# AdaLN beside w_out and the feed-forward network, in steps of four blocks

## The chip, the cores and the metric

The kernel runs on one core of one Trainium2 chip. The metric is the device time of one execution in microseconds (us). The engines of the core are TensorE (PE: matmuls and transposes; PEld: the loading of its stationary operand), VectorE (DVE), ScalarE (ACT), GpSimd (POOL) and SyncE (SP, which here issues the DMAs). Each works through a queue of its own in order, and semaphores tie the queues together.

## What is computed

Two layers of a diffusion backbone. Each layer normalises the tokens, modulates them, mixes them (a state space model, a neighbourhood attention and a grouped-query attention side by side), projects with w_out, and runs a gated feed-forward network. One tile of 128 prompt tokens and four tiles of sample tokens go through, with a width of 1024. Cut to what matters here:

```
m = silu(cond) @ w_ada + b_ada                 # 1024 -> 6 * 1024, for prompt and sample
sh1, sc1, g1, sh2, sc2, g2 = split(m, 6)
h = layer_norm(x) * (1 + sc1) + sh1
o = mixing(h) @ w_out
x = layer_norm(ALPHA * x + g1 * o, ln1_g, ln1_b)
h = layer_norm(x) * (1 + sc2) + sh2
a, gate = split(h @ w_ffn_in, 2)
x = layer_norm(ALPHA * x + g2 * ((silu(a) * gate) @ w_ffn_out), ln2_g, ln2_b)
```

The first three lines' `m` is what is called AdaLN below: six vectors (vec 0 to 5 for sh1, sc1, g1, sh2, sc2, g2) of 1024 numbers for each of two conditions, in each layer.

## The kernel before, in words

All large products are done in fp32 as three passes of matmuls over a high and a low part (`mm3`: lines L311, L312, L313). A weight comes from memory into a raw buffer, ScalarE casts its high part (L283) and GpSimd or VectorE subtracts it for the low part (L284, tile `wl`, `hl` or another).

**AdaLN.** `ada` makes one item: half a vector, 512 columns of `w_ada`. Its 1024 rows come as eight blocks of 128 rows x 512 columns (256 KB each, L377). Each block is multiplied by four small matmuls (L381), so 32 for an item, which add up in one PSUM bank; ScalarE copies the result out (L385), TensorE transposes it ("turns the row", L386), and VectorE adds the bias into `modc` (L391 or L393). After the second half of a gate (vec 2 or 5) the column copy `gc` (L396), another transpose (L398) and a store (L401) put the gate out as a row. With `side=True` the blocks come into the ring `ev` of four buffers, which also holds the low parts of some weights in the turn and the intermediate values of the SSM tables.

**The turn.** `wout` multiplies the groups of token tiles (2, 1, 0) and (3, 4) by w_out, for two halves `n` of the columns each; VectorE applies the gate (L1497) and the residual (L1303), then come the layer norm (L1288, L1298), the transposes to the network's input (L417), the modulation (L423) and differences and splits for the network (`ffn_in_tile`, L1545, L284). After the products of the second group, three items of `ada` are issued (`ADAW`): both halves of vec 5 of this layer, and, in layer 0 only, the first half of vec 0 of layer 1.

**The network.** Its hidden width is cut into 22 slices f = 0 to 21, in six parts of 4, 4, 4, 3, 4 and 3. The first two are "plain": their first halves need tiles 0, 1 and 2 only, their second halves (which end at L1711 and L1712) also tiles 3 and 4. The other slices use seven products of 12 matmuls in the manner of Strassen, with sums on VectorE (L1588 for weights, L1638, L1654 and L1656 for results in `ys`). After each part its w_ffn_out products follow. From f = 2 on each f is followed by one step of `ffn_side`: in layer 0 an item of `ada` for layer 1 (nine items) and a step of the SSM tables of layer 1 (`ssm_tables`: among others the products L615 and sums L617 in `ev`, stored as tabC). Layer 1 has no layer behind it, and so no side work in its network.

Which instruction stands where in an engine's queue is decided by a scheduler ahead of time, from the order of the code and its own estimates of durations; in the network, `issue_after(self.mark.ins)` keeps a side step behind the last VectorE product of its f.

## Time and profile before

| | us |
|---|---|
| three timed runs, median | 1805.65 |
| lowest and highest | 1800.99, 1809.15 |
| the profiled execution | 1804.75 |
| its span in the trace | 1802.7 |
| TensorE busy | 1655.2 (92% of the span) |
| VectorE busy | 1224.2 (68%) |
| ScalarE busy | 822.3 (46%) |
| GpSimd busy | 762.5 (42%) |

The span runs from the first to the last instruction that the profiler saw; 2.05 us of the profiled execution lie around it. Durations below are from this one execution.

### The profile page before, as it was taken

What the parts mean: (1) busy time and instruction counts of PE and PEld (TensorE: products, weight loads), DVE (VectorE), ACT (ScalarE), POOL (GpSimd) and SP (SyncE); (2) the same over time, 40 slices, a digit from 0 to 9 for tenths busy, and PEclk for the clock granted to TensorE, in tenths of its full rate; (3) what the DMA queues carried; (4) which work ended last, traced back from release to release, by engine and by line L of the source; (5) the groups of instructions that cost most, each with busy time, mean ns of one, the idle gap of its engine ahead of it and who ended that gap; (6) DMA issues with size and microseconds to landing.
All of it is one profiled execution on the core that took longest, in us unless ns stands there. A gap on an engine that the chain in (4) does not pass through costs nothing.

```text
span 1802.7 us, 31473 instructions
## 1 busy us (share of the span) xinstructions
PE 1655.2 (92%) x11624; PEld 1447.3 (80%) x11624; DVE 1224.2 (68%) x2460; ACT 822.3 (46%) x1796; POOL 762.5 (42%) x651
## 2 busy tenths in 40 slices
PE   5889899898899999999898989998979999999997
PEld 3778677676688888898797978976759898998995
DVE  5576536646778777678877555565476787876777
ACT  5435445556542334243246446665564342432433
POOL 3753303048434334346266232210684464363453
PEclk8889899889899999999999989998989999999999
DMA  8434767545453545332324243463542232222312
GB/s 311 121 110 116 231 202 203 149 158 178 149 161 115 176 126 184 109 115 72 122 77 165 91 115 86 121 183 113 178 161 83 91 98 64 89 74 68 105 60 82
DMA packets 183114, 234.90 MB, mean 130 GB/s; under 512 B 78960, under 2 KB 112048, under 8 KB 182960
## 3 DMA queue, kind: packets, MB, share of 16 engines
q1 hardware_dynamic: 182960, 232.88, 42.3%
q8 instruction: 92, 1.51, 0.3%
q14 instruction: 62, 0.51, 0.1%
HBM read 203.57 MB, written 29.39 MB: 129 GB/s over the span
## 4 chain that ended last, share of the span: by engine, by line
PE 66%; DVE 12%; DMA 10%; ACT 4%; issue 3%; POOL 2%; SPq 1%; POOLq 0%; DVEq 0%; ACTq 0%
PE psM L311 9%; PE psM L312 9%; PE psM L313 9%; PE psT L311 6%; PE psT L312 6%; PE psT L313 5%; DMA ev<-in_w_ada_dram 3%; PE psT L859 3%; PE psS L311 2%; PE psS L312 2%; PE psS L313 2%; PE psS L1157 2%; DMA wr<-in_w_ffn_in_dram 2%; PE psT L1184 2%; POOL wl L284 2%
## 5 line engine op out<-in xcount | busy, mean ns | idle before, releaser
L284 POOL TENSOR_TENSOR wl<-wr,wh 128x512 fp32r<-128x512 f32 x362 | 502.1, 1406 | 523.8 <-ACT wh L283 341.6
L283 ACT CAST wh<-wr 128x512 fp32r<-128x512 f32 x450 | 275.0, 620 | 388.4 <-PE psM L313 91.3
L311 PE MATMUL psM<-hh,wh 128*128 128x320 f32 x560 | 178.1, 318 | 2.5 <-DVE ev L400 1.2
L312 PE MATMUL psM<-hl,wh 128*128 128x320 f32 x560 | 176.2, 315 | 0.3 <-POOL hl L284 0.3
L313 PE MATMUL psM<-hh,wl 128*128 128x320 f32 x560 | 176.2, 315 | 0.0
L311 PEld LDWEIGHTS psM<-hh,wh 128*128 128x128 f32 x560 | 107.1, 191 | 5.5 <-DVE ev L400 1.8
L311 PE MATMUL psT<-hh,wh 128*128 128x320 f32 x352 | 110.0, 312 | 0.0
L312 PE MATMUL psT<-hl,wh 128*128 128x320 f32 x352 | 109.1, 310 | 0.0
L313 PE MATMUL psT<-hh,wl 128*128 128x320 f32 x352 | 109.0, 310 | 0.0
L313 PEld LDWEIGHTS psM<-hh,wl 128*128 128x128 f32 x560 | 107.0, 191 | 1.7 <-issue 1.6
L312 PEld LDWEIGHTS psM<-hl,wh 128*128 128x128 f32 x560 | 107.2, 191 | 1.1 <-POOL hl L284 0.6
L230 POOL TENSOR_TENSOR sm<-sm,mhalf 128x1 f32<-128x1 f32 (+2 forms) x46 | 55.9, 1217 | 96.3 <-DVE sm L260 51.7
L1638 DVE TENSOR_TENSOR ys<-ys,psM 128x320 f32<-128x320 f32 x140 | 65.0, 482 | 34.7 <-PE psM L313 32.9
L1638 DVE TENSOR_TENSOR ys<-ys,psT 128x320 f32<-128x320 f32 x140 | 65.1, 481 | 30.4 <-PE psT L313 29.0
L1160 DVE TENSOR_REDUCE psS<-psS 128x1 f32<-128x640 f32 x64 | 52.8, 828 | 45.3 <-PE psS L1157 43.7
L311 PE MATMUL psT<-b,wh 128*128 128x320 f32 x240 | 76.6, 319 | 7.3 <-DVE ys L1638 7.2
L311 PE MATMUL psM<-b,wh 128*128 128x320 f32 x240 | 76.4, 318 | 5.7 <-DVE ys L1638 5.6
L284 POOL TENSOR_TENSOR wl<-ws,wh 128x512 fp32r<-128x512 f32 x40 | 53.6, 1341 | 62.7 <-ACT wh L283 62.6
L311 PE MATMUL psM<-wh,hh 128*128 128x256 f32 (+1 forms) x232 | 73.8, 318 | 6.1 <-DVE sm L1329 2.9
L311 PE MATMUL psM<-wh,xs 128*128 128x512 f32 x190 | 75.1, 395 | 3.5 <-DVE k L1762 2.8
L311 PE MATMUL psT<-wh,xs 128*128 128x512 f32 x190 | 75.3, 396 | 2.9 <-DVE k L1762 2.9
L859 PE MATMUL psT<-ident,ys 128*128 128x128 f32 x440 | 75.4, 291 | 2.7 <-ACT ys L290 1.0
(439 smaller groups left out, 4904.8 us busy)
## 6 DMA issues: line engine op xcount, KB each, us to landing
wr<-in_w_ffn_in_dram SPq DMA_DIRECT2D x88, 512.0 KB, 3.8
ev<-in_w_ada_dram SPq DMA_DIRECT2D x112, 256.0 KB, 4.0
wr<-in_w_ffn_out_dram SPq DMA_DIRECT2D x40, 512.0 KB, 3.9
wr<-in_w_out_dram SPq DMA_DIRECT2D x32, 512.0 KB, 3.6
wr<-in_w_in_dram SPq DMA_DIRECT2D x28, 512.0 KB, 4.4
wa<-in_w_ada_dram SPq DMA_DIRECT2D x24, 512.0 KB, 4.6
k<-in_x_dram SPq DMA_DIRECT2D x10, 512.0 KB, 5.6
xs<-zqk SPq DMA_DIRECT2D x32, 160.0 KB, 5.1
```

The source lines that it names most:

```text
L230: self.nc.gpsimd.tensor_tensor(out=o, in0=v, in1=self.mhalf.broadcast_to([128, v.shape[1]]), op=ALU.pow)
L283: nc.scalar.copy(hi, src)
L284: (lo_eng or nc.vector).tensor_tensor(out=lo, in0=src, in1=hi.bitcast(F32), op=ALU.subtract)
L311: nc.tensor.matmul(ps, lhsT=ah, rhs=bh, start=first, stop=False)
L312: nc.tensor.matmul(ps, lhsT=ah, rhs=bl, start=False, stop=False)
L313: nc.tensor.matmul(ps, lhsT=al, rhs=bh, start=False, stop=last)
L859: self.nc.tensor.transpose(pt[:, j * 128:(j + 1) * 128], s, self.ident)
L1157: nc.tensor.matmul(sp[:, b, 0:320], lhsT=qT[:, h * 128:(h + 1) * 128], rhs=kx[kv][:, b * 320:(b + 1) * 320], start=st, stop=en)
L1160: V.tensor_reduce(out=m, in_=sp[:, :, 0:320], axis=AX.XY, op=ALU.max, negate=True)
L1184: nc.tensor.matmul(pt[hh * 64:hh * 64 + 64, 256:384], lhsT=K["v"][:, j, kv * 64:kv * 64 + 64], rhs=PTs[j // 2][:, c0:c0 + 128], start=(j = ...
L1638: V.tensor_tensor(out=o, in0=x, in1=y, op=ALU.add)
```

## The change

`ada` loses its side form. Side work is now done by `ada_steps`, a generator that works on half items of four blocks. One step does three things for three different half items: it turns the row of the one multiplied a step earlier (L416) and adds it into `modc` (L423 in the new code with the bias for the first half, L420 for the second); it multiplies the four blocks that the step before had loaded (16 matmuls, L433) and copies the result to the tile `zt` (two buffers) rather than to `ev`; and it issues four loads (L445) into the four buffers of `ev`.

In `wout` the generator gets the two items of vec 5, so four half items. It steps once ahead of the groups and once after each group's products of each half `n`, ahead of the gate and the residual; the rest is drained behind the groups. The ten items of layer 1 (twenty half items) go one step per f from f = 2 on, and what is left is drained ahead of the last part's w_ffn_out products. A side step in the network is now also held behind the last matmul that `mm3` has issued (`issue_after(self.last.ins)`). The core of the diff:

```diff
-    def ada(self, l, M, vec, half, wide=None, side=False):
+    def ada(self, l, M, vec, half, wide=None):
...
+    def ada_steps(self, items):
...
+        made = loaded = None
+        todo = [(*x, k0) for x in items for k0 in range(0, KD, 4)]
+        while todo or loaded or made:
+            if made or loaded:
+                bank = self.psS()[:, 0] if self.ada_wide else self.psM()
+            if made:
+                (l, M, vec, half, k0), mrow = made
+                pt = bank[:, 128:256]
+                nc.tensor.transpose(pt, mrow, self.ident)
+                mc = M["modc"][:, vec, half * 4:half * 4 + 4, :]
+                got = pt.rearrange("p (j r) -> p j r", j=4)[:, :, 0:2]
+                if k0:
+                    nc.vector.tensor_tensor(out=mc, in0=got, in1=mc, op=ALU.add)
+                else:
...
+                    nc.vector.scalar_tensor_tensor(out=mc, in0=got, scalar=float(vec in (1, 4)), in1=bc, op0=ALU.add,
+                                                   op1=ALU.add)
+                if (half, k0) == (1, 4) and vec in (2, 5):
+                    self.gate_rows(M, vec, bank, self.zt)
+                made = None
+            if loaded:
+                (l, M, vec, half, k0), raws = loaded
+                ps = bank[:, 0:128]
+                for k in range(4):
+                    for j in range(4):
+                        nc.tensor.matmul(ps[32 * j:32 * j + 32, :], lhsT=self.silc[:, k0 + k, :],
+                                         rhs=raws[k][:, j * 128:(j + 1) * 128], start=(k == 0), stop=(k == 3),
+                                         tile_position=(0, 32 * j))
+                mrow = self.zt(128)
+                nc.scalar.copy(mrow, ps)
+                made, loaded = (loaded[0], mrow), None
+            if todo:
...
+                raws = [self.ev() for _ in range(4)]
+                for k in range(4):
+                    nc.sync.dma_start(raws[k], wv[:, k0 + k, c0:c0 + 512])
+                loaded = item, raws
+            yield
...
-        ada = self.ada_side(l, M, nxt)
+        ada = self.ada_steps([(l, M, 5, half) for half in range(2)])
+        self.ada_wide = False
+        next(ada)
...
+                next(ada, None)
                 for p, i in zip(ps, group):
...
-            self.ada_wide = False
-            for _ in range(self.ADAW[min(self.GROUPS.index(group), 1)]):
-                next(ada, None)
-            self.ada_wide = True
...
-        return self.ffn(l, xs, M, H, nxt, ada)
+        for _ in ada:
+            pass
+        self.ada_wide = True
+        return self.ffn(l, xs, M, H, nxt, self.ada_side(l, nxt))
...
-                    with self.tc.issue_after(self.mark.ins):
+                    with self.tc.issue_after(self.mark.ins), self.tc.issue_after(self.last.ins):
                         next(side, None)
...
+            yield from self.ada_steps([(l + 1, M, vec, half) for vec in range(5) for half in range(2)])
```

The new code is 46 to 49 lines longer ahead of `wout`, so a line of before such as L423 (the modulation) is L469 in the changed kernel, L1303 is L1349, L1545 is L1592, L664 (the store of tabC) is L710, and L1582 (a load of w_ffn_in) is L1629.

**The end of w_out in layer 0.** TensorE's queue before, just behind the last product of w_out; `ev` are blocks, `xs` rows of a token tile that are transposed:

```order
1657 L381 MATMUL psM_5027<-ev_5046,silc 32x128 x4
1658 L381 MATMUL psM_5027<-ev_5052,silc 32x128 x4
1659 L381 MATMUL psM_5027<-ev_5058,silc 32x128 x4
1660 L381 MATMUL psM_5027<-ev_5064,silc 32x128 x4
1661 L381 MATMUL psM_5027<-ev_5070,silc 32x128 x4
1662 L417 MATMUL psT_4793<-ident,xs_4775 128x128 x4
1663 L417 MATMUL psT_4802<-ident,xs_4776 128x128 x4
1664 L386 MATMUL psM_5027<-ident,ev_5076 128x128
1665 L381 MATMUL psM_5080<-ev_5081,silc 32x128 x4
1666 L381 MATMUL psM_5080<-ev_5087,silc 32x128 x4
```

And the same place in the changed kernel:

```order
1667 L313 MATMUL psS_5027<-wh_5100,hl_3772 128x512
1668 L416 MATMUL psM_5116<-ident,zt_5013 128x128
1669 L463 MATMUL psT_4857<-ident,xs_4839 128x128 x4
1670 L463 MATMUL psT_4866<-ident,xs_4840 128x128 x4
1671 L433 MATMUL psM_5116<-ev_5015,silc 32x128 x4
1672 L433 MATMUL psM_5116<-ev_5016,silc 32x128 x4
1673 L433 MATMUL psM_5116<-ev_5017,silc 32x128 x4
1674 L433 MATMUL psM_5116<-ev_5018,silc 32x128 x4
1675 L416 MATMUL psM_5241<-ident,zt_5135 128x128
1676 L311 MATMUL psS_5278<-hh_3771,wh_5256 128x320
```

The 96 multiplies behind w_out have become 16, with two turns, and the first product of the network (row 1676) follows at once. VectorE's queue at the same place before; the residuals of tiles 3 and 4 are written to `k`:

```order
544 L1303 SCALAR_TENSOR_TENSOR k_886_4835,sm_4837<-k_886_4835,psS_4934 128x512
545 L1497 TENSOR_TENSOR psS_4934<-psS_4934,k_832_4560 128x512
546 L252 TENSOR_SCALAR sm_5198<-sm_4837 128x1
547 L1303 SCALAR_TENSOR_TENSOR k_888_4838,sm_4840<-k_888_4838,psS_4934 128x512
548 L423 TENSOR_SCALAR xs_4735<-psT_4753,modc_91 128x128 x3
549 L423 TENSOR_SCALAR xs_4736<-psT_4762,modc_91 128x128 x3
550 L252 TENSOR_SCALAR sm_5248<-sm_4840 128x1
```

And in the changed kernel:

```order
547 L469 TENSOR_SCALAR xs_4800<-psT_4826,modc_91 128x128 x3
548 L423 SCALAR_TENSOR_TENSOR modc_91<-psM_5116,bcol_89 128x8
549 L1546 TENSOR_TENSOR psS_5027<-psS_5027,k_842_4595 128x512
550 L1349 SCALAR_TENSOR_TENSOR k_902_4899,sm_4901<-k_902_4899,psS_5027 128x512
551 L469 TENSOR_SCALAR xs_4839<-psT_4857,modc_91 128x128 x3
552 L1546 TENSOR_TENSOR psS_5027<-psS_5027,k_842_4595 128x512
553 L252 TENSOR_SCALAR sm_5143<-sm_4901 128x1
554 L469 TENSOR_SCALAR xs_4840<-psT_4866,modc_91 128x128 x3
555 L420 TENSOR_TENSOR modc_91<-psM_5241,modc_91 128x8
556 L1349 SCALAR_TENSOR_TENSOR k_904_4902,sm_4904<-k_904_4902,psS_5027 128x512
```

Twelve modulation rows (two groups of three in each of tiles 0 and 1) and the add of the last turn (row 555) have moved ahead of the last residual (547 before, 556 now).

**The end of the network of layer 0.** TensorE's queue before, from the last product of f = 21 to the first of the last part's w_ffn_out:

```order
4276 L311 MATMUL psT_10355<-b_884_4819,wh_10260 128x320
4277 L312 MATMUL psT_10355<-b_885_4820,wh_10260 128x320
4278 L313 MATMUL psT_10355<-b_884_4819,wl_10261 128x320
4279 L311 MATMUL psS_10467<-wh_10378,xs_9968 128x512
4280 L312 MATMUL psS_10467<-wl_10379,xs_9968 128x512
```

And in the changed kernel:

```order
4277 L313 MATMUL psT_10364<-b_900_4883,wl_10270 128x320
4278 L416 MATMUL psS_10384<-ident,zt_10226 128x128
4279 L433 MATMUL psS_10384<-ev_10228,silc 32x128 x4
4280 L433 MATMUL psS_10384<-ev_10229,silc 32x128 x4
4281 L433 MATMUL psS_10384<-ev_10230,silc 32x128 x4
4282 L433 MATMUL psS_10384<-ev_10231,silc 32x128 x4
4283 L416 MATMUL psS_10447<-ident,zt_10403 128x128
4284 L433 MATMUL psS_10447<-ev_10405,silc 32x128 x4
4285 L433 MATMUL psS_10447<-ev_10406,silc 32x128 x4
4286 L433 MATMUL psS_10447<-ev_10407,silc 32x128 x4
4287 L433 MATMUL psS_10447<-ev_10408,silc 32x128 x4
4288 L416 MATMUL psS_10468<-ident,zt_10466 128x128
```

Two batches of multiplies stand there now, one right behind the other, with three turns; the second reads the blocks that go into the buffers which the first has read.

**The tables late in the network of layer 0.** SyncE's queue before, where tabC is stored:

```order
449 L1582 DMA wr_9263<-in_w_ffn_in_dram 128x1024
450 L1582 DMA wr_9421<-in_w_ffn_in_dram 128x1024
451 L1582 DMA wr_9423<-in_w_ffn_in_dram 128x1024
452 L1582 DMA wr_9581<-in_w_ffn_in_dram 128x1024
453 L664 DMA tabC_5862<-ev_9249 128x2x256
454 L664 DMA tabC_5862<-ev_9254 128x2x256
455 L1582 DMA wr_9583<-in_w_ffn_in_dram 128x1024
456 L664 DMA tabC_5862<-ev_9409 128x2x256
```

And in the changed kernel:

```order
437 L1629 DMA wr_9882<-in_w_ffn_in_dram 128x1024
438 L445 DMA ev_9297<-in_w_ada_dram 128x512
439 L710 DMA tabC_5775<-ev_9302 128x2x256
440 L445 DMA ev_9483<-in_w_ada_dram 128x512
441 L1629 DMA wr_9884<-in_w_ffn_in_dram 128x1024
442 L445 DMA ev_9484<-in_w_ada_dram 128x512
443 L710 DMA tabC_5775<-ev_9307 128x2x256
444 L445 DMA ev_9485<-in_w_ada_dram 128x512
445 L445 DMA ev_9486<-in_w_ada_dram 128x512
446 L1629 DMA wr_10059<-in_w_ffn_in_dram 128x1024
```

The loads of AdaLN now reach into these f's and alternate with the stores of the tables, in the same four buffers, with the next weights between them.

## Rows read from the trace of the kernel before

**Rows 1.** The page: busy time of each engine, and the last chain by engine.

```profile
PE 1655.2 (92%) x11624; PEld 1447.3 (80%) x11624; DVE 1224.2 (68%) x2460; ACT 822.3 (46%) x1796; POOL 762.5 (42%) x651
...
PE 66%; DVE 12%; DMA 10%; ACT 4%; issue 3%; POOL 2%; SPq 1%; POOLq 0%; DVEq 0%; ACTq 0%
```

**Rows 2.** Busy time by stretch: length; PE, PEld, DVE, ACT, POOL; granted clock; DMA.

```profile
425.00:515.00 90.00, 75.60 (x606) 62.79 (x605) 62.05 (x123) 48.57 (x93) 52.52 (x44) 0.89 0.48 151
515.00:960.00 445.00, 423.14 (x2859) 375.34 (x2858) 351.74 (x635) 164.46 (x329) 191.03 (x143) 0.99 0.42 128
1300.00:1390.00 90.00, 77.40 (x514) 64.76 (x513) 64.66 (x135) 53.91 (x102) 60.06 (x48) 0.91 0.40 131
443.20:482.10 38.90, 27.05 (x237) 19.94 (x241) 31.34 (x65) 23.29 (x46) 22.32 (x20) 0.74 0.56 183
1327.40:1366.30 38.90, 28.91 (x218) 22.51 (x219) 30.93 (x68) 24.06 (x48) 23.74 (x21) 0.78 0.50 169
```

**Rows 3.** TensorE's waits (us, times, longest): two from 425:515, one from 1290:1420.

```profile
PE psM L381 <- DMA ev<-in_w_ada_dram: 12.1, 7, 3.4
PE psM L398 <- DVE gc L396: 2.3, 1, 2.3
...
PE psM L381 <- DMA ev<-in_w_ada_dram: 8.2, 4, 3.5
```

**Rows 4.** TensorE's timeline in layer 0's turn: start, us, line, operation [idle before <-releaser].

```profile
448.49 1.26 PE L381 MATMUL psM<-ev,silc 128*32 128x128 f32 x16 [3.37 <-DMA ev<-in_w_ada_dram]
449.68 1.97 PE L417 MATMUL psT<-ident,xs 128*128 128x128 f32 x8
...
475.51 0.43 PE L381 MATMUL psM<-ev,silc 128*32 128x128 f32 x8 [3.17 <-DMA ev<-in_w_ada_dram]
...
481.80 0.64 PE L381 MATMUL psM<-ev,silc 128*32 128x128 f32 x16
```

**Rows 5.** VectorE's timeline in layer 0's turn.

```profile
443.21 0.69 DVE L1303 SCALAR_TENSOR_TENSOR k<-k,psS 128x512 f32<-128x512 f32 x1
...
444.93 2.00 DVE L423 TENSOR_SCALAR xs<-psT,modc 128x128 f32<-128x128 f32 x6 [1.02 <-ACT xs L425]
...
454.17 1.04 DVE L423 TENSOR_SCALAR xs<-psT,modc 128x128 f32<-128x128 f32 x3
...
502.92 0.49 DVE L1711 TENSOR_TENSOR psT<-ys,psT 128x320 f32<-128x320 f32 x1
```

**Rows 6.** GpSimd's timeline: tile 4's last split.

```profile
480.73 1.30 POOL L284 TENSOR_TENSOR hl<-ys,hh 128x512 fp32r<-128x512 f32 x1 [1.86 <-ACT hh L283]
```

**Rows 7.** VectorE's timeline in layer 1's turn.

```profile
1327.38 0.69 DVE L1303 SCALAR_TENSOR_TENSOR k<-k,psS 128x512 f32<-128x512 f32 x1
...
1381.28 0.49 DVE L1711 TENSOR_TENSOR psT<-ys,psT 128x320 f32<-128x320 f32 x1
```

**Rows 8.** TensorE's wait for blocks in the network of layer 0, 515:960.

```profile
PE psS L381 <- DMA ev<-in_w_ada_dram: 4.2, 8, 1.5
```

**Rows 9.** VectorE's timeline: table products of two of the four f's.

```profile
852.73 6.91 DVE L615 TENSOR_TENSOR ev<-k,k 128x512 f32<-128x512 f32 x4
...
884.94 2.50 DVE L615 TENSOR_TENSOR ev<-k,k 128x512 f32<-128x512 f32 x4
```

**Rows 10.** DMA issues: operation, times, KB each, median us to landing.

```profile
ev<-in_w_ada_dram SPq DMA_DIRECT2D x112, 256.0 KB, 4.0
...
tabC<-ev SPq DMA_DIRECT2D x8, 256.0 KB, 3.7
```

**Rows 11.** SyncE's timeline: six loads of blocks ahead of a weight's load.

```profile
486.55 21.50 SPq L377 DMA_DIRECT2D ev<-in_w_ada_dram  x6
```

**Rows 12.** TensorE's timeline: a transpose between products, and a whole item.

```profile
486.25 0.27 PE L386 MATMUL psM<-ident,ev 128*128 128x128 f32 x1
...
505.81 1.08 PE L381 MATMUL psS<-ev,silc 128*32 128x128 f32 x32
```

**Rows 13.** TensorE's timeline at the last part of layer 0's network.

```profile
956.28 0.50 PE L311 MATMUL psS<-wh,xs 128*128 128x512 f32 x1 [1.33 <-ACT xs L283]
```

More of the change, by code (lines that the diff above doesn't have):

```diff
@@ L312, in mm3 @@
         nc.tensor.matmul(ps, lhsT=ah, rhs=bl, start=False, stop=False)
-        nc.tensor.matmul(ps, lhsT=al, rhs=bh, start=False, stop=last)
+        self.last = nc.tensor.matmul(ps, lhsT=al, rhs=bh, start=False, stop=last)
     def setup(self):
@@ L364, in ada @@
         c0 = vec * D + half * 512
-        bank = self.psS()[:, 0] if side and self.ada_wide else self.psM()
+        bank = self.psM()
         ps, pt = bank[:, 0:128], bank[:, 128:256]
-        step = 1 if side or wide else 2
+        step = 1 if wide else 2
         for k0 in range(0, KD, step):
-            if side:
-                raw = self.ev().rearrange("p (k n) -> p k n", k=1)
-            else:
-                if wide:
-                    raw = wide[k0]()[:, 0:512].rearrange("p (k n) -> p k n", k=1)
-                else:
-                    raw = self.wp.tile([128, step, 512], F32, name=self.nm("wa"), tag="wr", bufs=self.NRAW)
+            if wide:
+                raw = wide[k0]()[:, 0:512].rearrange("p (k n) -> p k n", k=1)
+            else:
+                raw = self.wp.tile([128, step, 512], F32, name=self.nm("wa"), tag="wr", bufs=self.NRAW)
             nc.sync.dma_start(raw, wv[:, k0:k0 + step, c0:c0 + 512])
@@ L383, in ada @@
                                      tile_position=(0, 32 * j))
-        mrow = self.ev(n=128) if side else self.zt(128)
+        mrow = self.zt(128)
         nc.scalar.copy(mrow, ps)
@@ L394, in ada @@
         if vec in (2, 5) and half == 1:
-            gc = self.smallp.tile([128, 2, KD], F32, name=self.nm("gc"), tag="gc", bufs=1)
-            nc.vector.tensor_copy(gc, modc[:, vec].rearrange("p k c -> p c k"))
-            pt = bank[0:16, 256:384]
-            nc.tensor.transpose(pt, gc.rearrange("p c k -> p (c k)"), self.ident)
-            row = (self.ev(n=128) if side else self.zt(128))[0:16]
-            nc.vector.tensor_copy(row, pt)
-            nc.sync.dma_start(gates[vec // 3].rearrange("c (k p) -> (c k) p", p=128), row)
+            self.gate_rows(M, vec, bank, self.zt)
@@ new lines, in gate_rows @@
+    def gate_rows(self, M, vec, bank, place):
+        nc = self.nc
+        gc = self.smallp.tile([128, 2, KD], F32, name=self.nm("gc"), tag="gc", bufs=1)
+        nc.vector.tensor_copy(gc, M["modc"][:, vec].rearrange("p k c -> p c k"))
+        pt = bank[0:16, 256:384]
+        nc.tensor.transpose(pt, gc.rearrange("p c k -> p (c k)"), self.ident)
+        row = place(n=128)[0:16]
+        nc.vector.tensor_copy(row, pt)
+        nc.sync.dma_start(M["gates"][vec // 3].rearrange("c (k p) -> (c k) p", p=128), row)
@@ L1799, in ffn, with ada_side @@
             f0 += nf
-    def ada_side(self, l, M, nxt):
-        for half in range(2):
-            self.ada(l, M, 5, half, side=True)
-            yield
+    def ada_side(self, l, nxt):
         if l + 1 < L:
-            nxt["M"] = self.ada_begin(l + 1)
-            for vec in range(5):
-                for half in range(2):
-                    self.ada(l + 1, nxt["M"], vec, half, side=True)
-                    yield
+            M = nxt["M"] = self.ada_begin(l + 1)
+            yield from self.ada_steps([(l + 1, M, vec, half) for vec in range(5) for half in range(2)])
     def ffn_side(self, l, nxt, ada):
```

8 lines of the change are left out of this document (7 added, 1 removed).

## The prediction

> **What bounds the kernel now.** I read the page first. TensorE is busy 92% of the span, and two thirds of the chain of work that ended last lie on it; a tenth of that chain is DMA [rows 1]. Shares over the whole span hide where the idle time is, so the next view was busy time by stretch. The feed-forward network is nearly full; the turn from w_out into the network is not. In layer 0, from 425 to 515 us, TensorE is busy 75.60 of 90 us and its granted clock is 0.89; the next 445 us have 423.14 busy and 0.99. Layer 1 shows the same turn, 77.40 of 90 [rows 2]. The waits of that stretch say why: of 14.4 us of idle time in layer 0, 12.1 are TensorE waiting for AdaLN blocks, 7 times, and 2.3 for VectorE's column copy `gc`; layer 1 has 8.2 for blocks [rows 3]. The timeline shows the form: `ada` loads a block, multiplies it, loads the next, and TensorE's queue runs in order, so each late block (3.37 us, 3.17 us) holds everything behind it, the transposes of the token tiles among it [rows 4].
>
> So the edit aims at the right wait. What decides the result is what is late next. In the turn that is VectorE: from the last residual of w_out (443.21 us) to the end of tile 4's last split on GpSimd (480.73 + 1.30 = 482.03), VectorE is busy 31.34 of 38.9 us, and 30.93 of 38.9 in layer 1 [rows 2, 5, 6]. With no AdaLN wait at all, this stretch would still need some 31 us.
>
> **The change, part by part.** The profiled execution took 1804.75 us (span 1802.7 and 2.05 around it); the median of the three timed runs is 1805.65, 0.9 more. The sum stands on 1804.75.
>
> *Layer 0, the turn into the network.* Before, three items (of 32 multiplies and 8 loads each) stood behind the second group's products. Now vec 5 goes in four steps beside w_out's products, and only the fourth multiply and two turns stand at w_out's end. I price it in two ways. By items: layer 0 has three of them after w_out and needs 502.92 - 443.21 = 59.7 us from the last residual to the second end of the plain halves; layer 1 has two and needs 1381.28 - 1327.38 = 53.9 [rows 5, 7]. One item is thus worth 5.8 us, three 17.4. Against it stands a delay of the last residual. Three batches of 16 multiplies with their turns now lie among w_out's products: 0.64 us a batch at the full clock, 1.26 at the half [rows 4], so 1.9 to 3.8, taken 2.4. And in VectorE's queue the last turn's add now stands ahead of tile 4's last residual: it waits for eight transposes of a token tile on TensorE (1.97 us in this place before [rows 4]), 16 multiplies, ScalarE's copy and a transpose, 3.6 us as an estimate from those rows. Together 6, so 17.4 - 6 = 11.4 gained. By VectorE: of its 31.34 us, the 12 modulation rows of tiles 0 and 1 (six in 2.00 us, then two groups of three like the one of 1.04 [rows 5], 4.1 in all) move ahead of the last residual; 27.2 are left, with a microsecond for handovers 28; 38.9 - 28 - 6 = 5 gained. I take 8, between the two. The ends are 4 (VectorE's way, less one more handover) and 14.4 (all idle time of the stretch gone).
>
> *Layer 1, the same turn.* By items 2 x 5.8 - 6 = 5.6; by VectorE 38.9 - (30.93 - 4.1 + 1) - 6 = 5. Taken 5. The ends are 2 lost (the residual's delay not covered) and 8.2 gained (its waits for blocks gone [rows 3]).
>
> *The network of layer 0, what goes.* Between 515 and 960 us TensorE waited 4.2 us for blocks [rows 8]. The new steps issue their loads one f ahead, some 15 us (884.94 - 852.73 is two of them [rows 9]), against 4.0 us to landing [rows 10]: 4.2 gained; ends 0 and 4.2. In SyncE's queue the third f's weights stood behind blocks that waited for their buffers: six issues stretched over 21.50 us [rows 11]. Little of it reached TensorE: 1 gained, ends 0 and 4.
>
> *What comes in.* The third item moves from the turn into the network: 32 multiplies, 1.08 us [rows 12]. Twelve items are turned in halves, so there are 12 more transposes, copies and adds. A transpose between products has a record of 0.27 us [rows 12], part of which overlaps its neighbours: 12 x 0.27 = 3.2 at most, 12 x 0.1 taken, 1.2. The copies and adds lie on ScalarE and VectorE, busy 164.46 and 351.74 of 445 us in the network [rows 2], on nobody's path there; without that slack each would add its own few tenths of a microsecond.
>
> *The ring of four.* `ev` has four buffers. Before, a block left its buffer as soon as it was multiplied, and AdaLN was through by the ninth f of the side work, so the SSM tables had the ring to themselves from there. Now a step holds all four from its loads to its multiply one f later, for every f from 2 to 21, and the tables' groups must pass between a multiply and the next four loads. In the four f's that build tabC this is a serial chain: the multiply 0.64, four products (6.91 us in one group, 2.50 in another), two sums of the cheap product's size 1.25, the store 3.7, four loads 4.0 plus some 1.7 for their issues [rows 9, 10]: 18.2 or 13.8 us, against a spacing of 16.1 (852.73 to 884.94, two f's). That is 2.1 late at worst and nothing at best, for those four. Taken 4 lost in all; the ends are 0 and 14 (20 steps at 0.7). The 2.50 and the 6.91 are the same four instructions, the dear ones beside splits on GpSimd. The Trainium skill (Perfetto Trace Analysis, Optimizing Scalar/DVE Operations) says that GpSimd and VectorE share a read port, so that work moved between or beside them may not speed up; by it, a group that is shifted by one multiply could fall on either price, 4.4 us apart, and the term would be 0 or 8 for the four.
>
> *The end of the network of layer 0.* The step of the last f frees the ring, only then can the last four loads start, and their multiply stands in TensorE's queue ahead of the last part's products. Landing 4.0, issues, two batches and two turns make some 6.5 us; 1.33 of it TensorE waits there anyway for `xs` [rows 13]. Taken 5 lost; ends 3 and 7. Behind these loads on SyncE stand the next layer's fourth w_in block and its norm gains, wanted only later.
>
> Sum: -8 - 5 - 4.2 - 1 + 1.1 + 1.2 + 4 + 5 = -6.9. 1804.75 - 6.9 = 1798.
>
> **The rivals.** *TensorE's waits were the only limit* (faster). Both turns give back their idle time, 14.4 + 8.2 instead of 13, and the ring costs nothing: 1798 - 9.6 - 4 = 1784. For it: VectorE's rows of tile 4 came late because TensorE's transposes stood behind the wait of 3.17 [rows 4]. Against it: VectorE's 31 busy us. A second source lies in the clock: 16 multiplies took 1.26 us after a wait and 0.64 once the engine had run on [rows 4]; if the stretch's 75.60 busy us at 0.89 went at the full clock, 75.60 x 0.11 = 8 us more would go, which I leave to the end of the range. The Trainium skill (TensorE: Matmul & The Clock Gate, Part 1) says that the array runs at 1.2 GHz when idle and at 2.4 GHz under sustained load; the trace agrees with 1.26 against 0.64, and by that rule the removal of waits pays more than the waits themselves.
>
> *The ring starves TensorE* (slower). VectorE's queue is in order too: a table product that waits for a buffer stands ahead of the `ys` sums that free TensorE's banks. If each of 15 of the 20 steps costs what a block's wait cost in the turn, 12.1 / 7 = 1.7 us [rows 3], the ring costs 25.5 rather than 4: 1798 + 21.5 = 1819. It decides the sign, by over 0.5%, when the twenty steps cost over 1 us each (20 in all). For it: VectorE is busy 351.74 of 445 us there [rows 2], and the store of each table half, which waits for it, stands on SyncE ahead of the next weights. Against it: after every third or fourth f come w_ffn_out's products, in which the ring catches up.
>
> *The turn keeps its length* (no change): the delay of the last residual eats both gains, 13 us, as VectorE's chain merely starts later: 1798 + 13 = 1811. The same comes out if the steps' loads are late beside w_out, where SyncE holds them behind w_out's own blocks, so that the change doesn't do what it says.
>
> **How the numbers follow.** My forecast 0.40, the faster rival 0.28, the starved ring 0.20, the turn unchanged 0.12. The predicted time is the likeliest case, 1798, by itself 1790 to 1806. The range leaves out the outer part of both signed rivals: 1781 to 1816. 0.5% is 9 us, about what a measurement of this kernel can tell from no change. Faster by more (below 1796): the faster rival and a third of the forecast's spread, 0.40. Slower (above 1814): the starved ring, 0.19. Within it: 0.41.
>
> **What would show it.** In the turn, waits for blocks near zero and a granted clock near 1; the last residual some 6 us later after w_out's products, tile 4's last split some 5 earlier. Around 950 us, one wait for blocks of 4 to 6 us ahead of the last part. From 830 to 905 us, waits of the multiplies for DMA of some 2 us each. It is wrong if the turn's idle time stays and only changes its name from DMA to VectorE, or if waits for blocks appear at most f's.

## The result, and the profile of the changed kernel

The changed kernel takes 1826.36 us (median; 1825.0 to 1835.83) against 1804.43 for the kernel before on the same chip: a ratio of 1.0124, with a 95% interval of 1.009 to 1.0158. It is slower by 22 us; the prediction was 7 us faster, and its range ended at 1816. The profiled execution of it has a span of 1825.3 us, 22.6 more than that of before.

The page of the changed kernel, busy time of each engine and the last chain by engine. Nearly the same work is done, TensorE's share of the span fell by a point, and the chain's share on DMA went from 10% to 6% while VectorE's rose from 12% to 14% [rows 1]:

```profile
PE 1656.3 (91%) x11638; PEld 1455.6 (80%) x11638; DVE 1235.3 (68%) x2474; ACT 823.1 (45%) x1810; POOL 762.5 (42%) x651
...
PE 62%; DVE 14%; POOL 7%; DMA 6%; ACT 5%; issue 5%; SPq 1%; POOLq 0%; DVEq 0%; ACTq 0%
```

To see where the 22.6 us are I cut both traces at the same events on VectorE: the first and the last residual of w_out, the product that closes f = 1 (L1712 before), f = 9 and f = 21 (L1656), and the fifth residual of the last part of layer 0's network, the first one of its third token tile. Lengths of the stages in us:

| stage | before | after | difference |
|---|---|---|---|
| start to the first residual of w_out, layer 0 | 398.4 | 394.9 | -3.5 |
| first to last residual of w_out | 44.8 | 54.9 | +10.1 |
| last residual to f = 1 | 60.7 | 47.8 | -12.9 |
| f = 1 to 9 | 191.2 | 184.8 | -6.4 |
| f = 9 to 21 | 259.9 | 287.8 | +27.9 |
| f = 21 to the last part's fifth residual (the drain) | 15.5 | 23.8 | +8.4 |
| to the first residual of w_out, layer 1 | 311.9 | 308.9 | -3.0 |
| first to last residual, layer 1 | 45.0 | 55.2 | +10.2 |
| last residual to f = 1, layer 1 | 54.9 | 47.5 | -7.4 |
| to the end | 420.5 | 419.7 | -0.8 |

So the two turns, which the change was aimed at, come to -2.8 and +2.8: nothing. The loss lies in layer 0's network and, with 8.4 - 3.0 = 5.4 us net, in the drain behind it. The cut at f = 9 also moves work across it: AdaLN's steps now reach to f = 21. The next view counts that: busy time of TensorE by stretch for the multiplies of AdaLN alone, of the changed kernel (L433), f = 1 to 9 and 9 to 21:

```profile
497.60:682.40 184.80, 7.12 (x192) 5.05 (x192) 0.97 0.39 114
682.40:970.20 287.80, 17.06 (x384) 9.14 (x384) 0.95 0.42 131
```

and of the kernel before (L381), the same two stretches:

```profile
503.90:695.10 191.20, 19.95 (x448) 10.57 (x448) 0.99 0.51 152
695.10:955.00 259.90, 6.49 (x128) 2.58 (x128) 0.99 0.35 111
```

Both have 576 records in all, nine items of 64 (the trace has two records for each multiply). 256 records have moved behind f = 9, 8.6 us at 1.08 for 32, and some products of the f's shift across the cut as well. So the two rows are not to be read apart; what counts is their sum, f = 1 to 21: 451.1 before, 472.6 after, **21.5 us lost**. Of these stretches TensorE was busy 432.45 and 438.68 us in all, idle 18.65 and 33.9: 15.3 us are new idle time, 6.2 are busy time, at a granted clock that fell from 0.99 in both stretches to 0.97 and 0.95.

What the idle time waits for: TensorE's waits (us, times, longest) of the kernel before, from 600 to 905 us,

```profile
PE psM L311 <- DVE ys L1638: 4.8, 4, 2.7
PE psT L311 <- DVE ys L1638: 3.0, 1, 3.0
PE psM L311 <- DVE k L1762: 2.8, 2, 2.5
PE psS L381 <- DMA ev<-in_w_ada_dram: 2.0, 5, 0.8
```

and of the changed kernel in the same stretch:

```profile
PE psS L677 <- DVE ev L663: 11.8, 2, 6.0
PE psM L311 <- DVE ys L1685: 4.8, 1, 4.8
PE psT L311 <- DVE k L1809: 1.2, 1, 1.2
PE psS L433 <- DMA ev<-in_w_ada_dram: 1.0, 1, 1.0
```

Waits for blocks are down to 1.0. In their place stand two waits of some 6 us at L677, the matmuls that read a group of table products (L661) and their sums (L663). Before, the counterpart of this line (L631) never waits in f = 1 to 21. VectorE's timeline of the changed kernel shows the first of the two:

```profile
664.24 1.58 DVE L284 TENSOR_TENSOR xs<-ys,xs 128x320 fp32r<-128x320 f32 x1
666.25 1.26 DVE L1635 TENSOR_TENSOR ws<-wr,wr 128x512 f32<-128x512 f32 x1 [0.43 <-DMA wr<-in_w_ffn_in_dram]
...
670.33 4.63 DVE L661 TENSOR_TENSOR ev<-k 128x512 f32<-128x512 f32 x4
674.88 1.75 DVE L1635 TENSOR_TENSOR wr<-wr,wr 128x512 f32<-128x512 f32 x1
676.55 0.68 DVE L663 TENSOR_TENSOR ev<-ev,ev 128x512 f32<-128x512 f32 x1
```

and TensorE's timeline there:

```profile
665.51 1.08 PE L433 MATMUL psS<-ev,silc 128*32 128x128 f32 x32
677.38 0.61 PE L677 MATMUL psS<-k,ev 128*128 128x32 f32 x2 [6.05 <-DVE ev L663]
682.06 1.92 PE L677 MATMUL psS<-k,ev 128*128 128x32 f32 x8
822.07 1.08 PE L677 MATMUL psS<-k,ev 128*128 128x32 f32 x8
```

The AdaLN multiplies at 665.51 set four buffers of `ev` free; only behind them come the four products of the group (670.33), on a VectorE that is just then making the splits and weight sums of the same f (the buffers have been free since 666.59; the last 3.7 us the products wait for their place in VectorE's queue); and TensorE has the readers next in its queue. The same stands at two other places: multiplies at 768.35, products at 772.88 (again 4.63 us), a wait of 5.76 at L677; and multiplies at 937.41, products at 941.94 (4.63), where the sums of `ys` behind them come too late: 6.06 at a product of L311.

```profile
768.35 1.08 PE L433 MATMUL psS<-ev,silc 128*32 128x128 f32 x32
779.92 0.61 PE L677 MATMUL psS<-k,ev 128*128 128x32 f32 x2 [5.76 <-DVE ev L663]
...
937.41 1.08 PE L433 MATMUL psS<-ev,silc 128*32 128x128 f32 x32
949.29 0.63 PE L311 MATMUL psM<-b,wh 128*128 128x320 f32 x1 [6.06 <-DVE ys L1685]
```

In the kernel before the counterpart of the first group is made early; VectorE, then TensorE:

```profile
651.32 1.89 DVE L615 TENSOR_TENSOR ev<-k 128x512 f32<-128x512 f32 x3
656.15 0.68 DVE L615 TENSOR_TENSOR ev<-k 128x512 f32<-128x512 f32 x1
657.42 0.68 DVE L617 TENSOR_TENSOR ev<-ev,ev 128x512 f32<-128x512 f32 x1
```

```profile
674.45 0.41 PE L631 MATMUL psS<-k,ev 128*128 128x32 f32 x2
675.00 1.08 PE L631 MATMUL psS<-k,ev 128*128 128x32 f32 x8
```

Its last sum ends at 658.10 and is read at 674.45, 16 us later; in the changed kernel 676.55 + 0.68 is followed by 677.38 at once. The three waits make 17.9 us. Behind the first two the granted clock is 0.50 from 680 to 690 and from 780 to 790 us, half of full speed. The wait of 4.8 for a `ys` sum, at 601.36, is a fourth of the kind: ahead of that sum VectorE makes power products of the same tables, through `ev` too, with a weight sum among them (596.36 to 600.91). No run changes this place by itself; in `tabs_between`, below, the wait there is 2.4.

In layer 0's turn, TensorE's waits of the changed kernel from 425 to 515 us [rows 3]:

```profile
PE psT L463 <- DVE xs L469: 5.5, 2, 4.2
PE psT L463 <- ACT ys L273: 4.9, 1, 4.9
PE psM L311 <- DVE zt L401: 2.2, 1, 2.2
```

No block is waited for (12.1 us before). The waits are for VectorE's modulation rows and ScalarE's normalised rows. VectorE's timeline up to the last residual [rows 5]:

```profile
443.76 2.00 DVE L469 TENSOR_SCALAR xs<-psT,modc 128x128 f32<-128x128 f32 x6 [1.93 <-ACT xs L471]
...
446.48 0.69 DVE L1349 SCALAR_TENSOR_TENSOR k<-k,psS 128x512 f32<-128x512 f32 x1
...
449.73 0.16 DVE L420 TENSOR_TENSOR modc<-psM,modc 128x8 f32<-128x8 f32 x1
449.80 0.68 DVE L1349 SCALAR_TENSOR_TENSOR k<-k,psS 128x512 f32<-128x512 f32 x1
```

and TensorE's there [rows 4]:

```profile
444.96 2.04 PE L463 MATMUL psT<-ident,xs 128*128 128x128 f32 x8 [4.23 <-DVE xs L469]
446.93 1.53 PE L433 MATMUL psM<-ev,silc 128*32 128x128 f32 x32
448.85 0.33 PE L416 MATMUL psM<-ident,zt 128*128 128x128 f32 x1 [0.40 <-ACT zt L437]
```

The last residual, at 443.21 before, now comes at 449.80, behind the rows, the transposes, the multiplies and the turn. Not all of the 10.1 us arises there: w_out has ten residuals in a layer, and the eighth already comes 37.0 us behind the first, against 33.4 before.

### The profile page after: what moved, and what is told of

It is laid out like the page before. It is cut to its first block, busy times and chain, and to the rows that moved or that the text cites. A ratio compares the mean times of both kernels' runs of the same rounds, so it can differ in the third digit from the quotient of the medians.

```text
span 1825.3 us, 31541 instructions
## 1 busy us (share of the span) xinstructions
PE 1656.3 (91%) x11638; PEld 1455.6 (80%) x11638; DVE 1235.3 (68%) x2474; ACT 823.1 (45%) x1810; POOL 762.5 (42%) x651
## 4 chain that ended last, share of the span: by engine, by line
PE 62%; DVE 14%; POOL 7%; DMA 6%; ACT 5%; issue 5%; SPq 1%; POOLq 0%; DVEq 0%; ACTq 0%
PE psM L311 9%; PE psM L312 8%; PE psM L313 8%; PE psT L311 6%; PE psT L312 6%; PE psT L313 5%; POOL wl L284 3%; PE psT L905 3%; DMA wr<-in_w_ffn_in_dram 2%; PE psS L1203 2%; PE psT L1230 2%; DVE wr L1635 2%; PE psS L311 2%; PE psS L312 1%; PE psS L313 1%
## 5 line engine op out<-in xcount | busy, mean ns | idle before, releaser
L311 PE MATMUL psM<-hh,wh 128*128 128x320 f32 x560 | 180.0, 322 | 7.3 <-DVE zt L401 4.2
L311 PEld LDWEIGHTS psM<-hh,wh 128*128 128x128 f32 x560 | 108.0, 193 | 11.5 <-DVE zt L401 5.0
L311 PE MATMUL psT<-hh,wh 128*128 128x320 f32 x352 | 111.9, 318 | 3.7 <-DVE ys L469 2.6
L1685 DVE TENSOR_TENSOR ys<-ys,psM 128x320 f32<-128x320 f32 x140 | 64.9, 482 | 43.2 <-PE psM L313 41.1
L311 PE MATMUL psM<-b,wh 128*128 128x320 f32 x240 | 76.5, 319 | 11.3 <-DVE ys L1685 11.2
L1685 DVE TENSOR_TENSOR ys<-ys,psT 128x320 f32<-128x320 f32 x140 | 65.2, 482 | 29.9 <-PE psT L313 28.4
L311 PE MATMUL psT<-b,wh 128*128 128x320 f32 x240 | 77.2, 321 | 7.4 <-DVE ys L1685 7.4
L311 PE MATMUL psT<-wh,xs 128*128 128x512 f32 x190 | 75.0, 395 | 3.7 <-DVE k L1809 3.7
L311 PE MATMUL psM<-wh,hh 128*128 128x256 f32 (+1 forms) x232 | 73.2, 315 | 4.4 <-DVE ys L1300 2.6
L313 PE MATMUL psT<-b,wl 128*128 128x320 f32 x240 | 76.2, 317 | 0.2
```

What stands on the lines that cost most here:

```text
L311: nc.tensor.matmul(ps, lhsT=ah, rhs=bh, start=first, stop=False)
L313: self.last = nc.tensor.matmul(ps, lhsT=al, rhs=bh, start=False, stop=last)
L1685: V.tensor_tensor(out=o, in0=x, in1=y, op=ALU.add)
```

## The experiments

Two theories stood against each other at first: **the ring** (the loss lies in the network, where a step's four loads push the tables' products one f on) and **the turn** (the delay of the residuals eats the gain and more). Others came up on the way: the added hold behind the last product, the drain, the add of the last turn. Stages are given as in the table above; "f = 1 to 21" is the sum of its two rows.

**One half of the change alone.** In `turn_only` the turn is as in the changed kernel, and the network's ten items are done in the way of before, without the added hold; in `net_only` it is the other way round. `ada_old` is the `ada` of before.

```diff
-            yield from self.ada_steps([(l + 1, M, vec, half) for vec in range(5) for half in range(2)])
+            for vec in range(5):
+                for half in range(2):
+                    self.ada_old(l + 1, M, vec, half, side=True)
+                    yield
```

> Only the turn is changed: vec 5 goes in steps of four beside w_out, and the ten items of layer 1 are made in the network as before the change (one whole item per f, block by block). Theory, that the loss of the change lies in layer 0's network: TensorE reaches the end of f = 1 in layer 0 some 4 us earlier than before and in layer 1 some 2 us later, the network of layer 0 keeps its length but for one more item (1 to 3 us), so 1800 to 1807 us. Rival, that the turn costs by itself: over 1812.

```diff
-                next(ada, None)
...
+            if len(group) == 2:
+                self.ada_wide = False
+                for half in range(2):
+                    self.ada_old(l, M, 5, half, side=True)
+                self.ada_wide = True
```

> Only the network is changed: vec 5 is made as before the change, two items block by block behind w_out, and the ten items of layer 1 go in half items, one step per f, as in the changed kernel. Theory: the whole loss of some 30 us in layer 0's network is there, so 1824 to 1834 us, with the same waits of 5 to 6 us of TensorE for table sums and ys sums and the drain at its end. Rival, that the loss needs the turn's steps too (later loads from there): under 1815.

`turn_only` takes 1809.99 us, a ratio of 1.0019 (0.9987 to 1.005): no difference. Its turns are 102.7 and 102.8 us, those of the changed kernel 102.7 and 102.7; its f = 1 to 21 is 454.7. `net_only` takes 1829.63, 1.0135 (1.0101 to 1.0169), with 474.2 for f = 1 to 21. The loss is in the network and its drain alone. TensorE's waits of `net_only` from 515 us on show the same two lines as the changed kernel (L677 and L1685 there):

```profile
PE psS L722 <- DVE ev L708: 11.7, 2, 6.0
PE psM L311 <- DVE ys L1728: 11.1, 2, 6.5
```

`turn_only` is above the 1800 to 1807 expected, as its network needs 3.6 us more for the tenth item, not 1 to 3. `net_only` has one item less in layer 0's turn than the kernel before, and from its last residual to f = 1 it needs 56.7 against 60.7: an item is worth 4.0 us there.

**The tables between the multiply and the loads.** If the ring is the cause, it is by the order inside one f. In `tabs_between` the generator stops between the multiply and the next four loads, and the tables' work of that f stands there.

```diff
                 made, loaded = (loaded[0], mrow), None
+            if cut:
+                yield
             if todo:
...
-            a, b = next(ada, 0), next(tab, 0)
-            if a == 0 and b == 0:
+            a, b, c = next(ada, 0), next(tab, 0), next(ada, 0)
+            if a == 0 and b == 0 and c == 0:
```

> The changed kernel with one order changed: in each side step of the network the tables' step is taken between the multiply, which frees the ring, and the next four loads, so that a table group gets the ring in its own f and its matmuls stand one f behind it, as before the change. Theory, that a table group which slips by one f runs right ahead of the matmuls that read it: TensorE's two waits for table sums (6.05 and 5.76 us) and the half clock behind them go, the drain stays; 1800 to 1810 us. Rival, that holding all four buffers for a whole f starves the weights' loads on SyncE wherever the tables stand: 1820 or more. Rival, that VectorE has too much work at the start of an f: waits of TensorE for ys sums take the place of the others, 1815 or more.

1811.43 us, 1.0042 (1.0012 to 1.0072): two thirds of the loss are gone with this alone. f = 1 to 21 is 458.7 instead of 472.6, in a profiled execution (1818.92) that lies 7.5 above the median; what it still needs over the 451.1 of before, 7.6 us, no run divides. TensorE's waits of `tabs_between` from 600 to 905 us:

```profile
PE psS L433 <- DMA ev<-in_w_ada_dram: 3.7, 4, 1.8
...
PE psS L683 <- DVE ev L665: 0.4, 1, 0.4
```

The waits for the tables are 0.4 us instead of 11.8. Blocks, which now load later, are waited for 3.7 us: the small price that the prediction had looked for. By stretch (length; busy time of the engines; granted clock; DMA), the changed kernel and then `tabs_between`:

```profile
700.00:800.00 100.00, 94.24 (x637) 83.91 (x636) 66.70 (x105) 31.93 (x63) 33.59 (x25) 0.93 0.37 117
905.00:960.00 55.00, 48.94 (x330) 44.75 (x329) 44.74 (x62) 18.62 (x37) 30.43 (x22) 0.94 0.42 127
```

```profile
700.00:800.00 100.00, 99.53 (x708) 88.52 (x709) 76.14 (x123) 36.67 (x72) 35.49 (x26) 0.98 0.42 129
905.00:960.00 55.00, 54.96 (x386) 51.29 (x385) 39.99 (x60) 21.22 (x41) 28.82 (x22) 1.00 0.42 134
```

**The drain, the hold, an earlier turn.** `late_drain` moves the last steps of AdaLN behind the second tile's products of the last part; `no_last` takes the added hold away; `early_turn` makes one more step within the first group's products of w_out for each half `n`, two in all.

```diff
-                for _ in side:
-                    pass
...
+                    if m == 1:
+                        for _ in side:
+                            pass
```

> The changed kernel with the drain of the side work moved behind the second token tile's products of the last part. Theory: the last loads land beside these products, the 10 us that TensorE loses ahead of the last part shrink to under 2; with what was given back later (4 us) the gain is 5 to 9 us: 1817 to 1821. Rival, that the last part waits for w_in's weights or xs anyway: 1824 to 1828.

```diff
-                    with self.tc.issue_after(self.mark.ins), self.tc.issue_after(self.last.ins):
+                    with self.tc.issue_after(self.mark.ins):
```

> The changed kernel without the second hold on a side step in the network (behind the last matmul of its f); the hold behind the last VectorE product stays, as before the change. Theory, that the loss comes from the order of ring, tables and their matmuls: the same two waits for table sums and the same length of the network within 4 us, 1822 to 1830 us. Rival, that this hold pushes the side work into the busiest stretch of an f: the network gets 15 us shorter or more, under 1812.

```diff
+                    if j == 1 and len(group) == 3:
+                        next(ada, None)
```

> The changed kernel with two more steps inside the first group's products of w_out, so that vec 5 is multiplied and turned before the last products of w_out. Theory, that the last residual comes 10.2 us later because VectorE takes modulation rows and the last turn's add ahead of it: without the turn the delay falls to 4 to 7 us, and each turn gets 2 to 4 us shorter, together 4 to 8: 1818 to 1822 us. Rival, that the modulation rows alone make the delay: no change, 1824 to 1829.

`late_drain`: 1827.27 us, 1.0128 (1.0096 to 1.0161). The wait ahead of the last part is gone: from f = 21 to the first residual of that part it needs 3.4 us, against 13.3 in the changed kernel and 4.2 before. Some of it comes back behind the second tile's products, where the drain now stands (a wait of 2.7 for ScalarE's copy among it), so that the fifth residual is reached after 20.0 rather than 23.8. But the time does not fall: in its profiled execution f = 9 to 21 is 2.4 longer and the start 6.5 longer than in the changed kernel's. The profiles of all runs say more on this stage. From f = 21 to the first residual of w_out in layer 1 the six kernels with this drain need 330.2 to 338.4 us, the three with the late one (`late_drain`, and `tabs_late` and `all3` below) 323.8 to 328.1, the six with none 318.4 to 327.4. So the drain costs some us there and its later place gives them back; in the time of the whole kernel no run shows it. `no_last`: 1824.28, 1.0106 (1.0063 to 1.0149), with the wait at L677 still there (12.5 us in three); the hold is not the cause, though a microsecond or two for it is not excluded. `early_turn`: 1836.73, 1.0158 (1.0117 to 1.0199): no gain, and slower than either expectation; the last residual is still late by 9.3 us.

**Put together.** `tabs_late` has the edits of `tabs_between` and `late_drain`, `all3` that of `early_turn` too.

> Both edits to the network together: the tables' step between the multiply and the loads, and the drain behind the second token tile's products of the last part. Theory, that the two losses (13 us of the tables' slip, some 9 of the drain, part of it given back) are separate: 1811 less 4 to 9, 1802 to 1807 us, no longer told from the kernel before. Rival, that the drain's loss was hidden behind another wait: 1809 to 1813.

> The three edits together: early steps in the turn, tables between multiply and loads, late drain. If each acts where the theory puts it, 1796 to 1803 us, as fast as the kernel before or some us faster. Rival, that VectorE bounds the turn and the network's f's whatever the order of the side work: 1805 to 1812.

1813.9 us, 1.0049 (1.0021 to 1.0078), and 1813.65, 1.0037 (1.0015 to 1.0059). Neither goes below `tabs_between`, nor below the kernel before: with the ring mended, no form of the change that was tried here pays.

**No AdaLN at all.** How much was there to win? `no_ada` leaves AdaLN's work out of both turns and of the network; layer 1 and the second gate take layer 0's values.

```diff
-        ada = self.ada_steps([(l, M, 5, half) for half in range(2)])
+        ada = iter(())
...
-            yield from self.ada_steps([(l + 1, M, vec, half) for vec in range(5) for half in range(2)])
+            nxt["M"] = self.M0
+            yield from ()
```

> The floor: the changed kernel with AdaLN left out of both turns and of the network (vec 5 of either layer and all of layer 1's vectors are not computed, layer 1 and the second gate reuse what layer 0 has). What is left in these stretches is w_out, the norms, the network and the tables. Theory, that VectorE bounds the turn: from the first residual of w_out to the end of f = 1 it needs 100 to 103 us in both layers, as the changed kernel does (102.7 in both) and little less than before (105.5 and 99.9); the network from f = 1 to f = 21 needs 446 to 450 (451.1 before, 472.6 in the changed kernel). In all 1788 to 1800 us. Rival, that the steps themselves cost in the turn: under 97 us a turn, under 1788 us.

1774.08 us, 0.983 (0.9807 to 0.9852). From the first residual to f = 1 it needs 96.5 us in layer 0 and 97.9 in layer 1, against 105.5 and 99.9 before. With no AdaLN work whatever, the turns are 9.0 and 2.0 us shorter, and f = 1 to 21 11.4. TensorE's waits of `no_ada` in layer 1's turn, 1290 to 1420 us:

```profile
PE psT L463 <- ACT xs L273: 10.9, 1, 10.9
PE psT L463 <- ACT ys L273: 2.2, 1, 2.2
```

Where no block is waited for, one wait of 10.9 us for a normalised token tile takes its place. `no_ada` is no strict floor, as its queues are ordered anew: `before_12` below does the work of AdaLN and needs 97.2 us in layer 1's turn.

**Which part of the turn delays the residual.** `held_turn` is the changed kernel with the last multiply and both last turns held behind the last residual.

```diff
-        for _ in ada:
-            pass
+        with self.tc.issue_after(self.res.ins):
+            for _ in ada:
+                pass
```

> The changed kernel with the last multiply and both last turns of vec 5 held behind the last residual of w_out on VectorE. Theory, that the last turn's add ahead of the last residual makes most of its delay of 10.2 us (the stretch with no AdaLN has 2.5): 10.2 falls to 3 to 6, and the stretch from the first residual to the end of f = 1 from 102.7 to 97 to 100 in both layers: 1816 to 1821 us. Rival, that the modulation rows ahead of it make the delay: 8 or more stay, 102 or more, no change.

1827.68 us, 1.0142 (1.0091 to 1.0194). The adds of both last turns now stand behind the last residual, as VectorE's timeline of `held_turn` shows for the first of them, and the stretch from first to last residual is 54.9 in layer 0 all the same (in layer 1 it fell from 55.2 to 50.9):

```profile
445.30 2.15 DVE L469 TENSOR_SCALAR xs<-psT,modc 128x128 f32<-128x128 f32 x6 [1.93 <-ACT xs L471]
...
451.34 0.68 DVE L1349 SCALAR_TENSOR_TENSOR k<-k,psS 128x512 f32<-128x512 f32 x1
451.94 0.17 DVE L423 SCALAR_TENSOR_TENSOR modc<-psM,bcol 128x8 f32<-128x8 f32 x1
```

So it is not the add, in layer 0 at least. The modulation rows, with their own wait for ScalarE, remain ahead of the residual; but in `no_ada` they stand there too, and the stretch is only 2.5 longer than before. The eighth residual tells a part: it comes 37.0 us behind the first in the changed kernel and in `held_turn`, 33.4 in `no_ada` and before, with TensorE busy all the time. So 3.7 of the 10.1 us go with AdaLN's batches and turns among w_out's products, 2.5 are there without AdaLN too, and how the other 4 divide stays open.

**The kernel before with its items placed otherwise.** `ADAW` says how many items follow the first and the second group.

```diff
-    ADAW = (0, 3)
+    ADAW = (0, 2)
```

> The kernel before with two items behind w_out rather than three in layer 0; the third goes into the network, one item per f for ten f's. From the runs with one part changed: layer 0's turn 4.0 us shorter, the network 3.6 longer, so 1801 to 1807 us, no change. Rival, that an item is worth what two layers' difference says (5.8 us) and hides in the network: 1798 to 1800.

```diff
-    ADAW = (0, 3)
+    ADAW = (1, 2)
```

> The kernel before with one item behind the first group's products and two behind the second's. Theory, that the load waits of block-by-block items fall on TensorE wherever they stand: the item in front costs some 4 us among the products and gives back 4 behind them, no change within 5 us. Rival, that VectorE's norms hide it behind the first group: 4 to 8 us faster, as the two turns get one item shorter each.

```diff
-    ADAW = (0, 3)
+    ADAW = (2, 1)
```

> The kernel before with two items behind the first group's products of w_out and one behind the second's, so that in layer 1 nothing stands behind the second. One item in front made layer 0's turn 7.2 and layer 1's 4.9 us shorter (98.3 and 95.0 from the first residual to the end of f = 1). Theory, that w_out's second group hides loads and that what is hidden once cannot be hidden twice: layer 0 between 96 and 99, layer 1 between 94 and 97, in all within 4 us of one item in front, 1784 to 1792. Rival, that each item moved gives 5 us more: 1778 to 1782.

`before_02` (one item fewer in the turn, one more in the network): 1803.96 us, 0.999 (0.9971 to 1.001). From last residual to f = 1 it needs 55.6 in place of 60.7, with the same 44.8 from first to last residual; so this turn gives back 5.1, more than the 2.8 of the changed kernel. Layer 1's turn, with the same items as before, took 103.5 against 99.9: so far apart lie equal turns in different kernels.

`before_12` is **faster than both kernels: 1787.55 us, 0.9902 (0.9879 to 0.9926)**. That is more than either expectation. One item stands behind the first group and multiplies beside w_out, and TensorE waits for blocks less. Its waits from 385 to 510 us, and its busy time from 425 to 515 [rows 2, 3]:

```profile
PE psM L381 <- DMA ev<-in_w_ada_dram: 5.2, 3, 4.2
```

```profile
425.00:515.00 90.00, 81.57 (x616) 71.64 (x615) 67.04 (x137) 52.76 (x105) 60.03 (x47) 0.91 0.45 147
```

12.1 us of waits have become 5.2, and the turns are 98.3 and 97.2 us: 7.2 and 2.7 less than before, about what `no_ada` has (the 95.0 and 4.9 that the expectation of `before_21` gives for layer 1 count from the second residual). f = 1 to 21 stays at 451.6, since nothing touches the ring. Of the 15.2 us between the two profiled spans, 9.9 are the turns'; 5.0 come from the stage between f = 21 and layer 1's w_out, which does the same work, and `before_21` (1793.78, 0.9935, 0.991 to 0.996) has most of its gain there and at the start, with turns of 103.7 and 100.2. Why these stages are shorter the runs don't tell.

## Why the prediction was wrong, step by step

**The step that failed is the ring's term: 4 us, with ends of 0 and 14, where the network lost 21.5.** With the network's other terms the forecast was +1.1 us for f = 1 to 21. Of the 29.5 us between the forecast of -6.9 and the +22.6 of the two profiled spans, 20.4 lie here, 13.0 in the turns, 0.4 in the drain, and -4.3 in the start and the end. The ring's premise held: a group of products must pass between a multiply and the next four loads. But I asked only when the loads would come late, so I priced a serial chain against the spacing of two f's and looked for waits of the multiplies for DMA, some 2 us each from 830 to 905. There is none in that stretch, and one of 1.0 in the whole network, at 815.88. What I did not ask is who reads the group. Its readers stand in TensorE's queue at a fixed place, and before the group had been ready 16 us ahead of them [rows 9 show only its price]. The ring took this lead away at three places, 6.05, 5.76 and 6.06 us, 17.9 in all; behind the first two came some 10 us each at half the clock. That `tabs_between`, which moves nothing but the tables' place between multiplies and loads, brings f = 1 to 21 from 472.6 to 458.7 shows this cause for 13.9 of the 21.5 us.

**The rival "the ring starves TensorE"** (1819) had the sign, and its mechanism in half: a table product that waits for a buffer, ahead of the `ys` sums. Its price came from block waits in another stage, 15 times 1.7; the real ones are three of six. Its argument for w_ffn_out's products as a place to catch up did not bear on it, as it was not the loads that came late.

**The turns: -8 and -5 predicted, -2.8 and +2.8 measured.** That the waits for blocks go was right (12.1 to nothing), and so was that VectorE would be late next. Two sizes were off. The last residual came 10.1 and 10.2 us later in relation to the first, not 6. And an item was worth 4.0 (`net_only`) to 5.1 (`before_02`), not 5.8, so that the way by items gave too much. A third slip lies in the rows: I read 32 records as an item's 32 multiplies [rows 12], but the trace has two records for each. A batch of 16 is 1.08 us at the full clock, not 0.64, and an item 2.16; three batches cost 3.2 where I took 2.4, and the third item in the network twice the 1.1 I gave it. (The transposes, copies and adds that come in are 14, not 12, by the counts of the two pages.) In layer 1 the 5 us were not there to be had in this form: without any AdaLN the turn is 2.0 us shorter, and no run made it more than 2.7 shorter. The 8.2 us of waits for blocks [rows 3] lay in front of a wait of like length for a normalised tile; `no_ada` shows it, 10.9. The text had named this as what would make it wrong: the idle time stays and changes its name, there to VectorE, here to VectorE and ScalarE. The third rival (the turn keeps its length) is what both turns did.

**The network's small terms.** The waits for blocks went as predicted, 4.2 to 1.0. They brought nothing visible: from f = 1 to 9 TensorE's waits for `ys` sums rose from 2.1 to 11.3 us meanwhile. The weights' microsecond can't be told apart in these runs.

**The drain: 5 predicted, 8.4 measured** up to the fifth residual of the last part, beyond the end of 7; 3.0 of it are given back by layer 1's w_out, which the forecast had no term for, so that the net of 5.4 is near it partly by luck. The wait for blocks that was to show it is not named in the trace: TensorE waits 2.9 us for ScalarE's copy and 1.9 for a VectorE add there, while the last four loads, issued from 971.26 on, are on their way (the last eight loads take 4.2 us to landing in the median).

**The clock.** The faster rival counted on a higher clock in the turn (0.89 before), and the text looked for one near 1; it is 0.91 from 425 to 515 us in the changed kernel:

```profile
425.00:515.00 90.00, 73.01 (x470) 65.74 (x469) 69.18 (x134) 51.18 (x100) 56.27 (x45) 0.91 0.29 95
```

## What to carry to other kernels

Before a transfer is prefetched a step ahead, list everyone who uses its buffers: to hold a ring from one step to the next costs its other users a step, and the price is set by the reader of *their* results, not by the transfer. Where it must be, let the other users pass between the release and the next loads. And before a wait is priced as gain, ask what the same engine would wait for if it were gone; a run that leaves the work out helps to answer that, and here it said 2 us where the waits said 8.

## What had not been expected of the hardware

Four products of 32 columns at L677 (eight records, two for each product) took 1.92 us behind the wait of 6.05 (682.06) and 1.08 at 822.07, where only a wait of 1.2 stands ahead; the granted clock around the first, from 680 to 690 us, is 0.50, and that of 700 to 800 us is 0.93, against 0.98 in `tabs_between` without these waits. The prediction had counted the clock as a gain in the turn, not as a price in the network: of the 21.5 us lost, 6.2 are busy time. The Trainium skill (TensorE: Matmul & The Clock Gate, Part 1) has the array at 1.2 GHz when idle and 2.4 GHz under sustained load; the ratio of 1.92 to 1.08, with the waits ahead of the dearer one, is in line with that.

Four table products of 128x512 took 4.63 us at each of the three places above, beside splits on GpSimd, between the 2.50 and the 6.91 of before [rows 9]; at 906.62 two of them beside such splits took 2.38. Two ends seen in one trace were not the only prices.
